# Two-layer trunk with a hierarchical mixture of experts: three quads' outputs exchanged by DRAM rows, and the routing instructions beside it

## The chip, the cores and the metric

The kernel runs on one core of one Trainium2 chip. The time is that of one execution in device microseconds; the time before is the median of three runs. The four engines that the text speaks of are TensorE (PE in the rows; PEld is its weight load), VectorE (DVE), ScalarE (ACT) and GpSimd (POOL); SyncE (SP) issues weight transfers.

## The reference, cut to what matters

Two trunk layers run one after the other. Layer 0 has 512 tokens (256 latent ones, 256 context ones) of width 1024; in layer 1 only the 256 latent tokens are left. Each layer ends in the mixture of experts that the change is about: every token picks one of four groups of experts and in it the best two of four experts.

```python
def hier_moe(h, w_grp, b_grp, w_rtr, b_rtr, w_gate, w_up, w_down):
    p_grp = jax.nn.softmax((h @ w_grp + b_grp).astype(jnp.float32), axis=-1)
    pg, g = lax.top_k(p_grp, 1)
    ...
    pe, ie = lax.top_k(jax.nn.softmax(logits_sel, axis=-1), TOP_K_IN_GROUP)
    wts = pg * pe / jnp.sum(pe, axis=-1, keepdims=True)
    eid = g * EXPERTS_PER_GROUP + ie
    gates = jnp.sum(jax.nn.one_hot(eid, N_EXPERTS, dtype=jnp.float32) * wts[..., None], axis=1).astype(h.dtype)
    y = jnp.zeros_like(h)
    for e in range(N_EXPERTS):
        a = jax.nn.silu(h @ w_gate[e]) * (h @ w_up[e])
        y = y + gates[:, e:e + 1] * (a @ w_down[e])
    return y
...
        out = hier_moe(jnp.concatenate([h2, h2c], axis=0), *moe_args)
        x = x + g2 * out[:B * N].reshape(B, N, D)
        xc = xc + cg2 * out[B * N:].reshape(B, L, D)
```

The residual streams are x (latent, `xl` in the kernel) and xc (context); g2 and cg2 are columns of `modT`.

## The kernel before, in words

The 16 experts are handled as four quads of four (one routing group each), in an order found at run time (`place`). A quad has slots instead of tokens: 64 for each expert make two slot tiles of 128, and a third tile takes what overflows, 32 more for each expert. The third tile is worked only if the quad has such tokens (`more[q] > 0`, the branch `beyond(q)`); with these inputs the second and the third quad have it.

The **routing gap** lies ahead of the experts. VectorE finds each token's two experts (`choose`), its rank among the tokens of that expert (`rk`) and from both the number of its slot (`Routing.slots`, L917), makes one-hot matrices `OH` of them (`one_hot`, L1060), and TensorE multiplies the normed tokens, split in a high and a low half (`h2h`, `h2l`), by OH to get the first quad's input `XT` (`gather`, L780). Most of these small VectorE instructions show line L89, that of a helper. The normed tokens are also written to DRAM, `h2d` (L778).

In `experts` (L1098) each quad runs through

- the gate and up phases: four weight chunks of 2 MB each (L1096 holds every expert matmul), in which the slots' columns are the stationary side and the weights are streamed; the results are in PSUM (`acc`, `aux`);
- `slots` and `fetch` (L1116, L1129): VectorE makes the slot table `SS` of a quad (for each slot the tokens that are in it, as 0 and 1) and from it the token number of each slot; POOL fetches those rows of h2d by indirect DMA (`xg`), and `turn` transposes them into the next quad's XT, PSUM being emptied half by VectorE, half by ScalarE (L1154);
- `gates` (L1169): each slot's factor;
- `down`: four weight chunks of 2 MB, in two halves of 512 columns; the outputs `da` stay in PSUM, slots by columns;
- `halves` and `combine` (L1293, L1312), the **exchange**: `da` is split into `oh` (ScalarE, L1299) and `ol` (VectorE, L1300), and TensorE multiplies both by the slot table SS (L1317), which turns slots into token columns and sums a token's two experts of the quad; `add` (L1328) adds the result into X with the modulation's factor. In quads 0 to 2 the first half's exchange stands between the second half's weight chunks, the second half's in the next quad's gate phase (`pending`).

The last quad of layer 0 does its down phase in three parts: columns 0 to 512 with two chunks, and 512 to 768 and 768 to 1024 with a column piece each (`columns`, L1106: two DMAs of 1 MB). In this text the four weight buffers of that phase are its first to fourth down piece.

All weights of a layer come on SP's queue into a ring of five buffers, with `slot0` as a sixth, each of 2 MB; a transfer is issued when the buffer that it overwrites has been read. The order on each engine is made by a scheduler, except for what `keep_in_program_order` pins (and what goes through `pinned(V)`).

Of the kernel before, what the change touches and what calls it, by code (L numbers as in the profile page):

```python
# [14 lines left out]
I32 = mybir.dt.int32  # L15
# [22 lines left out]
CAP = {0: 96, 1: 64}  # L38

# [4 lines left out]
CO_ID, CO_ONE, CO_TOK, CO_SLOT, CO_BEFORE, CO_BASE, CO_QUAD, CO_FIRST = 0, 128, 256, 768, 788, 804, 836, 840  # L44
CO_W = 844
# [11 lines left out]
def build(tc, ctx, a, cap=CAP):  # L57
# [9 lines left out]
    gd = dram.tile([T, 4], F32, name="gd")  # L67

# [101 lines left out]
    def transpose(out, in_):  # L170
        PE.transpose(out, in_, ident)  # L171
# [630 lines left out]
    class Route:  # L802


        def __init__(self, l, nt, small, rt):
            self.l, self.nt, self.rt = l, nt, rt
            self.small, self.used = small.tile([P, 130 * nt], F32, name="small"), 0
            self.vec = small.tile([P, 4, nt], F32, name="vec")
            self.gov = small.tile([P, nt, 16], F32, name="gov")
            self.flag = small.tile([P, 1], I32, name="flag")  # L810
            self.plan = small.tile([P, 8], I32, name="plan")
# [105 lines left out]
        def slots(self, rk):  # L917
# [14 lines left out]
                             m.rearrange("p (m c) -> p m c", c=16), axis=AX.X, op=ALU.add)  # L932

# [164 lines left out]
    def experts(l, nt, h2, vec, gov, fv, place, more, XT, xpool, pool, where, last, begun):  # L1098
# [45 lines left out]
        def turn(xg, XT):  # L1144

            for i in range(2):
                for st in range(nst):
                    tp = tmp()
                    for c in range(4):
                        transpose(tp[:, c * P:(c + 1) * P], xg[st][0][:, (i * 4 + c) * P:(i * 4 + c + 1) * P])  # L1150
                    d, s_ = XT[:, i * 4:i * 4 + 4, st * P:(st + 1) * P], tp.rearrange("p (c t) -> p c t", c=4)
                    if st % 2:
                        for c in range(4):
                            S.activation(d[:, c, :], s_[:, c, :], AF.Identity, bias=modT[0][:, 24 + i * 4 + c, 0:1])  # L1154
                    else:
                        V.tensor_tensor(d, s_, modT[0][:, 24 + i * 4:28 + i * 4, 0:1].to_broadcast([P, 4, P]), op=ALU.add)
                    yield
# [50 lines left out]
        if l == 0:  # L1208
            x8 = slot0[0].tile([P, 2048], F32, tag="x", name="x8")
            yg = itertools.cycle([x8[:, 1536:1792], x8[:, 1792:2048]])  # L1210
        pending = []
        sq = []
        quad = [0]
        for q in range(4):
# [4 lines left out]
            for ch in range(4):  # L1219
# [30 lines left out]
            elif q == 0:  # L1250
                gts = gates(0), gates(1)
                gt = gts[0]
# [40 lines left out]
            def halves(da, c0=0, c1=512, parts=None):  # L1293
# [13 lines left out]
                return parts  # L1307

# [38 lines left out]
            if q < 3:  # L1347
# [8 lines left out]
            else:  # L1356
# [4 lines left out]
                for c0, c1 in itertools.pairwise(cuts):  # L1361
# [6 lines left out]
                    else:  # L1368
# [6 lines left out]
                        down(da[hf], 0, w[:, :, :, c0 % 256:c0 % 256 + m], *cols)  # L1375
                    if ready:
# [17 lines left out]
    for l in range(L):  # L1394
# [79 lines left out]
        if l == 0:  # L1474
# [10 lines left out]
            rt.rows(rs)  # L1485
            place, more = ro.order()
# [29 lines left out]
        with phase(f"ex{l}") as pool:  # L1516
            where = itertools.cycle([ring] * 5 + ([spare] * EXTRA + early if l else slot0))
            nxt = experts(l, nt, None if l == 0 else h2, vec, gov, fv, place, more, XT, hp, pool, where, l == L - 1, begun)
# [6 lines left out]
def constants():  # L1525
# [14 lines left out]
    co[:, CO_FIRST:CO_FIRST + 4] = [-100, 1, 2, 3]  # L1540

# [103 lines left out]
```

## Time and profile before

| | |
|---|---|
| median of three runs | 918.75 us (917.89 to 919.88) |
| the profiled execution, whole | 920.78 us |
| its span in the trace | 919.0 us, mean granted clock 0.988 |
| layer 0's experts on TensorE | 248 to 541 us |
| bytes moved by DMA | 287.22 MB |

The rows further down come from the profiled execution, in microseconds from its span's start. In a row of the timeline the start and the duration come first, then the engine, the line, the operation, what it writes from what, how many like it follow at once, and in brackets the idle time before it and what ended it. In rows of waits the waiting engine and line stand left of the arrow, what it waited for right of it. PEq and SPq are the engines' sequencers.

### The profile page before, as it was taken

The page shows a single profiled execution, that of the slowest core. Times are in us where ns is not written, and L with a number is a line of the kernel's source. Part 1 is how long each engine was busy: PE and PEld are TensorE (multiplying, and loading weights), DVE is VectorE, ACT ScalarE, POOL GpSimd, SP SyncE. Part 2 cuts the span into 40 slices and gives each one's busy share as a digit, 9 for nine tenths or more (in the row PEclk, how much of TensorE's full clock was granted, in tenths as well). Part 3 has the DMA queues.
Part 4 walks back from the last instruction along what each step waited for, and adds up shares of the span by engine and source line. Part 5 has one row for each costly group of instructions (what it writes and reads, how often), then busy time and mean ns, then how long its engine had stood idle before and what let it go on. Part 6 is the DMA issues. An engine that isn't in the chain of part 4 may idle for free. (4 is left out here: it accounts for less than half of the span.)

```text
span 919.0 us, 13230 instructions
## 1 busy us (share of the span) xinstructions
PE 862.8 (94%) x5082; PEld 477.6 (52%) x5082; DVE 406.9 (44%) x1038; ACT 270.1 (29%) x598; POOL 59.5 (6%) x71
## 2 busy tenths in 40 slices
PE   3899999999998999999999989999999999979998
PEld 2588666676543323442343358666963444324435
DVE  1466677823875322240330159777553232212212
ACT  3344667514521100110120156567331111100101
POOL 1000000111010120011000020000000000000000
PEclk9999999999999999999999989999999999999999
DMA  9645663653989999679878945957969999999971
GB/s 358 283 179 208 257 267 115 251 227 112 385 342 430 424 422 428 257 270 409 333 284 345 326 161 224 425 245 280 361 276 358 417 431 426 428 406 431 424 247 47
DMA packets 33618, 287.22 MB, mean 313 GB/s; under 512 B 3580, under 2 KB 13564, under 8 KB 17024
## 3 DMA queue, kind: packets, MB, share of 16 engines
q1 hardware_dynamic: 29168, 276.94, 74.9%
q0 software_dynamic: 2400, 7.89, 2.2%
q10 hardware_dynamic: 1968, 1.32, 0.5%
q8 instruction: 49, 0.80, 0.3%
q14 instruction: 33, 0.27, 0.1%
HBM read 282.97 MB, written 3.16 MB: 311 GB/s over the span
## 5 line engine op out<-in xcount | busy, mean ns | idle before, releaser
L1096 PE MATMUL acc<-w,XT 128*64 128x512 f32 (+1 forms) x768 | 168.3, 600 | 7.4 <-PEq L998 5.8
L1096 PE MATMUL aux<-w,XT 128*64 128x512 f32 (+1 forms) x512 | 106.7, 593 | 0.6 <-PEq L1190 0.6
L1096 PEld LDWEIGHTS acc<-w,XT 128*64 128x64 f32 (+1 forms) x768 | 50.7, 133 | 106.2 <-issue 103.9
L1096 PEld LDWEIGHTS aux<-w,XT 128*64 128x64 f32 (+1 forms) x512 | 33.0, 130 | 66.0 <-issue 65.2
L1096 PE MATMUL acc<-w,x 128*64 128x512 f32 (+2 forms) x272 | 53.8, 574 | 2.6 <-PEq L1190 2.3
L192 PE MATMUL aux<-w,c 128*32 128x512 f32 x368 | 46.8, 625 | 0.0
L115 DVE TENSOR_TENSOR wl<-w,wh 128x768 fp32r<-128x768 f32 (+2 forms) x48 | 44.9, 977 | 2.0 <-PE aux L192 1.0
L1274 DVE SCALAR_TENSOR_TENSOR sg<-aux,gt,sg 128x512 f32<-128x512 f32 x12 | 9.0, 750 | 80.1 <-PE aux L1096 79.4
L1300 DVE TENSOR_TENSOR ol<-acc,oh 128x512 fp32r<-128x512 f32 (+1 forms) x25 | 15.7, 627 | 59.8 <-ACT oh L1299 59.7
L137 PE MATMUL acc<-wh,hh 128*128 128x512 f32 x96 | 38.8, 404 | 2.3 <-ACT hh L300 2.2
L1299 ACT CAST oh<-acc 128x512 fp32r<-128x512 f32 (+1 forms) x25 | 13.4, 535 | 93.5 <-PE acc L1096 93.4
L115 ACT CAST wh<-w 128x768 fp32r<-128x768 f32 (+2 forms) x48 | 37.5, 831 | 7.0 <-DMA w<-w_pf 3.9
L139 PE MATMUL acc<-wh,hl 128*128 128x512 f32 x96 | 38.8, 404 | 0.0
L138 PE MATMUL acc<-wl,hh 128*128 128x512 f32 x96 | 38.3, 399 | 0.0
L1239 ACT ACTIVATE sg<-acc 128x512 f32<-128x512 f32 x16 | 9.4, 597 | 87.0 <-PE acc L1096 86.7
L525 ACT ACTIVATE pr<-acc,soft 128x512 f32<-128x512 f32 (+1 forms) x48 | 29.5, 620 | 11.9 <-DVE soft L522 11.9
L1096 PEld LDWEIGHTS acc<-w,x 128*64 128x64 f32 (+1 forms) x272 | 15.5, 130 | 32.4 <-issue 31.6
L1154 ACT ACTIVATE XT<-tmp,modT 128x128 f32<-128x128 f32 x24 | 7.0, 368 | 78.3 <-PE tmp L171 78.2
L1096 PE MATMUL aux<-w,aT 128*64 128x512 f32 (+2 forms) x192 | 29.1, 453 | 0.0
L1096 PE MATMUL acc<-w,aT 128*64 128x512 f32 (+1 forms) x160 | 28.8, 511 | 0.2 <-DVE aT L1271 0.2
L574 PE MATMUL aux<-pT,vt 128*64 128x128 f32 x320 | 27.5, 282 | 0.1
L1082 PE MATMUL tmp<-OH,h 128*128 128x256 f32 x104 | 23.8, 383 | 2.5 <-DVE OH L1065 2.0
(322 smaller groups left out, 1555.6 us busy)
## 6 DMA issues: line engine op xcount, KB each, us to landing
w<-wg SPq DMA_DIRECT2D x32, 2048.0 KB, 12.8
w<-wu SPq DMA_DIRECT2D x32, 2048.0 KB, 11.6
w<-wd SPq DMA_DIRECT2D x29, 2048.0 KB, 12.9
w<-w_mod SPq DMA_DIRECT2D x23, 2048.0 KB, 10.1
w<-w_out SPq DMA_DIRECT2D x4, 2048.0 KB, 7.8
w<-wd SPq DMA_DIRECT2D x6, 1024.0 KB, 12.8
w<-w_qkv SPq DMA_DIRECT2D x3, 1536.0 KB, 9.3
w<-w_pf SPq DMA_DIRECT2D x2, 2048.0 KB, 8.4
```

Of the source, the lines that this page charges most:

```text
L115: return S.copy(hi, x), eng.tensor_tensor(lo, x, hi.bitcast(F32), op=ALU.subtract)
L137: PE.matmul(out, lhs[0], rhs[0], start=start, stop=False, skip_group_check=True)
L138: PE.matmul(out, lhs[0], rhs[1], start=False, stop=False, skip_group_check=True)
L139: PE.matmul(out, lhs[1], rhs[0], start=False, stop=stop, skip_group_check=True)
L192: mm = PE.matmul(m[32 * j:32 * j + 32, :], sc2[:, k, :], w[:, kk, j * 512:(j + 1) * 512], start=(ch == chs[0] and kk == 0), stop=(ch == ch ...
L525: S.activation(pr[e], sp[e], AF.Exp, bias=nm[:, e:e + 1], scale=SCALE, accum_out=sums[:, e:e + 1])
L574: PE.matmul(o[e * 64:(e + 1) * 64, c * P:(c + 1) * P], vt[:, k0 + m, e * 64:(e + 1) * 64], pTs[e * nk + m], start=(m == 0), stop=(m == nk ...
L1082: PE.matmul(y[:, :W], x[:, tt, k * P:(k + 1) * P], OH[tt][:, c0:c1], start=(i == 0 and tt == 0), stop=(x is h2[-1] and tt == nt - 1))
L1096: PE.matmul(o, lhs[:, c0:c0 + m], w[:, j, :], start=(k == 0), stop=(k == last_k), skip_group_check=True)
L1239: S.activation(t, ga[st], AF.Silu)
L1299: S.copy(oh, da[st][:, c0:c1])
L1300: V.tensor_tensor(ol, da[st][:, c0:c1], oh.bitcast(F32), op=ALU.subtract)
```

## The change

In layer 0, quads 0 to 2 lose `halves` and `combine`. In their place `store` copies each of the three slot tiles' outputs from PSUM (ScalarE, for the second tile VectorE) and POOL's queue writes 256 KB for each and each half to rows of a DRAM tensor `yd`, six for a quad; a quad without third tile writes its first tile there instead. Row q x 384 + slot holds a slot's output, row 1152 zeros. In the routing gap `places` works out, for each token and each of its two experts, the number of that row; an expert of the last quad, or none, gives the row of zeros.

In the last quad's down phase `collect` fetches the two rows of each token, 128 tokens at a time, with two indirect DMAs of 512 KB, adds them on VectorE, transposes the sum in eight pieces on TensorE and adds them into X: the first two tiles of tokens around columns 0 to 512, the other two around columns 512 to 768. The last quad's own outputs go through `halves` and `combine` as before.

Also: quad 0 gets no slot table; the tables of the quads behind the second are pinned; the second quad's gates are written later; `turn` empties PSUM by VectorE alone.

```diff
 def slots(self, rk):
...
+            if l == 0:
+                self.ranks = self.rt.work[:, 560:560 + nt * 16]
+                S.copy(self.ranks, rk[:, 0:nt * 16])
+
+        def places(self):
...
+            V.tensor_tensor(b, self.base, c16[1], op=ALU.add)
+            V.tensor_scalar(t, r, 64.0, None, op0=ALU.is_ge)
+            V.tensor_tensor(t, t, c16[0][:, None, :].to_broadcast([P, nt, 16]), op=ALU.mult)
+            V.tensor_tensor(t, t, r, op=ALU.add)
+            V.scalar_tensor_tensor(t, self.ov, 1e6, t, op0=ALU.mult, op1=ALU.add)
+            V.tensor_tensor(t, t, b[:, None, :].to_broadcast([P, nt, 16]), op=ALU.add)
+            V.tensor_tensor(m.rearrange("p (i t) c -> p i (t c)", i=2), self.M.rearrange("p (i t) c -> p i (t c)", i=2),
+                            t.rearrange("p t c -> p (t c)")[:, None, :].to_broadcast([P, 2, nt * 16]), op=ALU.mult)
+            V.tensor_reduce(f, m, axis=AX.X, op=ALU.add)
+            V.tensor_scalar(self.rows, f, float(YD), None, op0=ALU.min)
...
-                V.tensor_scalar(t, bc[0], s_, None, op0=ALU.is_equal)
+                i = V.tensor_scalar(t, bc[0], s_, None, op0=ALU.is_equal)
+                if l == 0 and q > 1:
+                    tc.keep_in_program_order(i)
...
-                    if st % 2:
-                        for c in range(4):
-                            S.activation(d[:, c, :], s_[:, c, :], AF.Identity, bias=modT[0][:, 24 + i * 4 + c, 0:1])
-                    else:
-                        V.tensor_tensor(d, s_, modT[0][:, 24 + i * 4:28 + i * 4, 0:1].to_broadcast([P, 4, P]), op=ALU.add)
+                    V.tensor_tensor(d, s_, modT[0][:, 24 + i * 4:28 + i * 4, 0:1].to_broadcast([P, 4, P]), op=ALU.add)
...
+            z = pool.tile([P, D], F32, tag="xg", name="z", bufs=3)
+            G.memset(z[0:1, :], 0.0)
+            G.dma_start(yd[YD:YD + 1, :], z[0:1, :])
+        def collect(tts):
+
+            for tt in tts:
+                g = [pool.tile([P, D if tag == "xg" else nst * 512], F32, tag=tag, name="yr", bufs=3 if tag == "xg" else 2)[:, 0:D]
+                     for tag in (("xg", "xg"), ("oh", "ol"), ("xg", "SS"), ("xg", "xg"))[tt]]
+                for i in range(2):
+                    G.indirect_dma_start(out=g[i], out_offset=None, in_=yd[:, :],
+                                         in_offset=bass.IndirectOffsetOnAxis(ap=places[:, i * nt + tt:i * nt + tt + 1], axis=0))
+                tc.keep_in_program_order(V.tensor_tensor(g[0], g[0], g[1], op=ALU.add))
+                for i in range(2):
+                    t = tmp()
+                    for c in range(4):
+                        tc.keep_in_program_order(
+                            transpose(t[:, c * P:(c + 1) * P], g[0][:, (i * 4 + c) * P:(i * 4 + c + 1) * P]))
+                    for c in range(4):
+                        k = i * 4 + c
+                        x = X[tt // 2][:, k, tt % 2 * P:tt % 2 * P + P]
+                        V.scalar_tensor_tensor(x, t[:, c * P:(c + 1) * P], modT[l][:, 40 + k, tt // 2:tt // 2 + 1], x,
+                                               op0=ALU.mult, op1=ALU.add)
...
-                    SS, _ = slots(0, False)
+                    SS = None if l == 0 else slots(0, False)[0]
...
-                gts = gates(0), gates(1)
-                gt = gts[0]
+                gt = gates(0)
...
+            if l == 0 and q == 0:
+                gts = gt, gates(1)
...
+            def store(da, hf):
+
+                ys = pool.tile([P, nst, 512], F32, tag=("oh", "ol")[hf], name="ys", bufs=2)
+
+                def put(st, y):
+                    r0 = q * 384 + st * P
+                    G.dma_start(yd[r0:r0 + P, hf * 512:(hf + 1) * 512], y)
+
+                for st in range(2):
+                    (V.tensor_copy if st else S.copy)(ys[:, st, :], da[st])
+                    put(st, ys[:, st, :])
+                with beyond(q) as there:
+                    S.copy(ys[:, 2, :], da[2])
+                    put(2, ys[:, 2, :])
+                with there.Else():
+                    put(2, ys[:, 0, :])
...
-            if q < 3:
+            if l == 0 and q < 3:
+                for hf in range(2):
+                    for c in range(2):
+                        down(da[hf], 2 * c, weights(wd(l, place[q], 2 * hf + c)))
+                    store(da[hf], hf)
+            elif q < 3:
...
+                    if l == 0 and c0 < 768:
+                        collect(range(c0 // 256, c0 // 256 + 2))
...
             rt.rows(rs)
+            ro.places()
             place, more = ro.order()
```

**TensorE, first quad's down phase.** Before, ahead of and inside the second half's weights (x is the activations' transpose; xg the fetched rows; a branch row is that of the third tile):

```order
L1096 MATMUL acc<-w,x_2503 64x512 x8
L171 MATMUL tmp<-co,xg 128x128 x3
L1317 MATMUL tmp<-SS,oh 128x512
L1317 MATMUL tmp<-SS,ol 128x512
L1317 MATMUL tmp<-SS,oh 128x512
L1317 MATMUL tmp<-SS,ol 128x512
L1322 COMPARE_AND_BRANCH
```

And with the change, the same place:

```order
L1124 MATMUL acc<-w,x_2515 64x512 x7
L1370 COMPARE_AND_BRANCH
L1370 UNCONDITIONAL_BRANCH x2
L1124 MATMUL acc<-w,x_2515 64x512
L173 MATMUL tmp<-co,xg 128x128
L1124 MATMUL acc<-w,x_2515 64x512 x2
L1124 MATMUL aux<-w,x_2515 64x512 x2
```

The exchange's matmuls are gone from between the weight matmuls, and nothing takes their place there.

**TensorE, last quad's down phase with the change**, from the second down piece to the first exchange (yr is the sum of two fetched rows):

```order
L1124 MATMUL acc<-w,x_2515 64x512 x8
L173 MATMUL tmp<-co,yr 128x128 x8
L1124 MATMUL acc<-w,x_2515 64x256 x2
L1124 MATMUL aux<-w,x_2515 64x256 x2
...
L1124 MATMUL aux<-w,x_2515 64x256
L173 MATMUL tmp<-co,yr 128x128 x8
L1124 MATMUL aux<-w,x_2515 64x256
L1384 MATMUL acc<-SS,oh 128x512
```

The first token tile's eight transposes stand ahead of the third down piece, the second's inside it; the third's and the fourth's follow among the exchange's matmuls, ahead of the fourth piece.

**POOL, from the third quad's last stores on, with the change** (ys is the stored copy):

```order
L1365 DMA yd<-ys 128x512 x2
L1246 DMA yr<-yd,rows 128x1024 x4
L917 TENSOR_LOAD plan
L1216 COMPARE_AND_BRANCH
L1216 UNCONDITIONAL_BRANCH x2
L1246 DMA yr<-yd,rows 128x1024 x2
...
L1246 DMA yr<-yd,rows 128x1024
...
L1246 DMA yr<-yd,rows 128x1024
```

Six of the eight fetches follow the stores at once; the last token tile's two come one by one, the second of them after the first tile's transposes have freed the buffer that it is written to.

**VectorE, routing gap, with the change** (L951 to L957 are of `places`; small and rw are its work space):

```order
L91 TENSOR_SCALAR small<-acc 128x64
L951 TENSOR_TENSOR rw<-rw,co 128x16
L91 SCALAR_TENSOR_TENSOR rw<-small,rw 128x64
...
L952 TENSOR_SCALAR rw<-rw 128x64
L91 TENSOR_REDUCE vec<-rw 128x8
L953 TENSOR_TENSOR rw<-rw,co 128x64
L91 TENSOR_SCALAR sj<-names,vec 128x256
L954 TENSOR_TENSOR rw<-rw 128x64
L91 SCALAR_TENSOR_TENSOR OH<-names,vec,sj 128x256
...
L955 SCALAR_TENSOR_TENSOR rw<-small,rw 128x64
```

Four of the nine instructions stand ahead of the first one-hot matrix, the others between the later ones; seven are ahead of the last piece of h2l.

## Rows read from the trace of the kernel before

**Rows 1.** The page, part 1: busy time and share of the span.

```profile
PE 862.8 (94%) x5082; PEld 477.6 (52%) x5082; DVE 406.9 (44%) x1038; ACT 270.1 (29%) x598; POOL 59.5 (6%) x71
```

**Rows 2.** Table by stretch: us, TensorE busy (instructions), granted clock, DMA share, GB/s.

```profile
276.00:523.00 247.00, 236.40 (x1268) 1.00 0.90 361
288.00:317.00 29.00, 25.56 (x112) 1.00 1.01 428
448.00:484.00 36.00, 35.65 (x195) 1.00 0.72 277
```

**Rows 3.** Waits, TensorE, 276 to 523 us: total, times, longest us.

```profile
PE acc L1096 <- PEq L1190: 1.8, 4, 0.5
```

**Rows 4.** Waits, SP's DMA queue, 240 to 545 us.

```profile
SPq L108 <- PE acc L1096: 88.5, 15, 11.6
SPq L108 <- PE aux L1096: 85.5, 17, 11.0
```

**Rows 5.** Table by stretch, of L1317, the exchange matmuls, alone (PE, then weight loads).

```profile
299.70:321.40 21.70, 9.77 (x32) 5.39 (x32) 1.00 1.01 426
377.70:404.40 26.70, 12.38 (x48) 8.62 (x48) 1.00 0.68 261
461.40:488.10 26.70, 12.39 (x48) 8.61 (x48) 1.00 0.68 260
```

**Rows 6.** Groups by form, 276 to 545 us: busy us, mean ns of one.

```profile
L1156 DVE TENSOR_TENSOR XT<-tmp,modT 128x512 f32<-128x512 f32 x12 | 8.0, 689 | 17.2 <-PE tmp L171 17.2
...
L1299 ACT CAST oh<-acc 128x512 fp32r<-128x512 f32 x13 | 7.6, 586 | 44.1 <-PE acc L1096 44.1
L1174 DVE SCALAR_TENSOR_TENSOR sk<-bc,co,bg 128x1024 f32<-128x1024 f32 x6 | 7.4, 1279 | 0.2 <-DVEq L1278 0.2
...
L1154 ACT ACTIVATE XT<-tmp,modT 128x128 f32<-128x128 f32 x24 | 7.0, 368 | 78.3 <-PE tmp L171 78.2
...
L1337 DVE SCALAR_TENSOR_TENSOR xl<-tmp,modT,xl 128x256 f32<-128x256 f32 x12 | 5.8, 481 | 9.0 <-PE tmp L1317 9.0
```

**Rows 7.** Timeline, TensorE: start, us, instruction.

```profile
363.42 1.06 PE L171 MATMUL tmp<-co,xg 128*128 128x128 f32 x8 [0.83 <-PE tmp L171]
```

**Rows 8.** Timeline, TensorE in the routing gap.

```profile
239.07 2.14 PE L791 MATMUL acc<-OH,h2h 128*128 128x256 f32 x16 [1.83 <-DVE OH L89]
...
248.19 2.37 PE L1096 MATMUL acc<-w,XT 128*64 128x512 f32 x10
```

**Rows 9.** Timeline, VectorE in the routing gap.

```profile
235.32 0.17 DVE L89 TENSOR_SCALAR rw<-tmp 128x16 f32<-128x16 f32 x1 [0.42 <-PE tmp L858]
...
237.73 0.29 DVE L89 TENSOR_REDUCE vec<-rw 128x8 f32<-128x128 f32 x1
```

**Rows 10.** Timeline, POOL.

```profile
253.59 0.76 POOL L778 DMA_DIRECT2D h2d<-xt  x1 [0.51 <-DVE small L89]
267.59 1.43 POOL L1140 DMA_INDIRECT xg<-h2d,ii  x1 [13.24 <-PEq L1190]
```

**Rows 11.** Line L778, the write of h2d: its landing.

```profile
DMA to landing us min/median/max: 7.4/8.6/9.7
```

**Rows 12.** Timeline, TensorE, end of the last quad.

```profile
523.63 0.60 PE L1096 MATMUL aux<-w,x 128*64 128x256 f32 x4
...
532.30 0.65 PE L1096 MATMUL acc<-w,x 128*64 128x256 f32 x4
...
543.89 1.16 PE L270 MATMUL acc<-co,part 128*128 128x1 f32 x8 [2.55 <-POOL part L261]
```

**Rows 13.** Timeline, SP, the last quad's column pieces.

```profile
502.51 12.29 SPq L1110 DMA_DIRECT2D w<-wd  x4
```

**Rows 14.** Line L1140, the indirect fetches: landing.

```profile
DMA to landing us min/median/max: 9.8/16.0/22.3
```

**Rows 15.** Table by stretch: all engines, granted clock behind the last quad.

```profile
545.00:551.50 6.50, 5.38 (x25) 3.64 (x24) 3.80 (x9) 1.42 (x3) 0.00 (x0) 0.50 0.00 0
```

**Rows 16.** Timeline, TensorE, transposes of the first fetched tiles.

```profile
293.07 1.06 PE L171 MATMUL tmp<-co,xg 128*128 128x128 f32 x8 [1.37 <-DMA xg<-h2d,ii]
```

More of the change, by code (lines that the diff above doesn't have):

```diff
@@ L38 @@
 CAP = {0: 96, 1: 64}
+YD = 3 * 384
 PAR_BMOD, PAR_NG, PAR_WR, PAR_BR, PAR_PSC = 0, 96, 128, 448, 488
 PAR_W = 492
-CO_ID, CO_ONE, CO_TOK, CO_SLOT, CO_BEFORE, CO_BASE, CO_QUAD, CO_FIRST = 0, 128, 256, 768, 788, 804, 836, 840
-CO_W = 844
+CO_ID, CO_ONE, CO_TOK, CO_SLOT, CO_BEFORE, CO_BASE, CO_QUAD, CO_FIRST, CO_ROW = 0, 128, 256, 768, 788, 804, 836, 840, 844
+CO_W = 876
 MC_ROT, MC_MASK = 0, 512
@@ L67, in build @@
     gd = dram.tile([T, 4], F32, name="gd")
+    yd = dram.tile([YD + 1, D], F32, name="yd")
     def phase(name, side="left"):
@@ L170, in transpose @@
     def transpose(out, in_):
-        PE.transpose(out, in_, ident)
+        return PE.transpose(out, in_, ident)
     def keep_warm(n, bank=tmp):
@@ L810, in __init__ @@
             self.flag = small.tile([P, 1], I32, name="flag")
+            self.rows = small.tile([P, 2 * nt], I32, name="rows") if l == 0 else None
             self.plan = small.tile([P, 8], I32, name="plan")
@@ L932, in slots @@
                              m.rearrange("p (m c) -> p m c", c=16), axis=AX.X, op=ALU.add)
+            if l == 0:
+                self.ranks = self.rt.work[:, 560:560 + nt * 16]
+                S.copy(self.ranks, rk[:, 0:nt * 16])
+        def places(self):
+            nt = self.nt
+            c16 = [co[:, CO_ROW + i * 16:CO_ROW + (i + 1) * 16] for i in range(2)]
+            r = self.ranks.rearrange("p (t c) -> p t c", t=nt)
+            w = self.rt.work[:, 324:]
+            b = w[:, 0:16]
+            t = w[:, 16:80].rearrange("p (t c) -> p t c", t=nt)
+            m = w[:, 80:208].rearrange("p (m c) -> p m c", c=16)
+            f = w[:, 208:208 + 2 * nt]
+            V.tensor_tensor(b, self.base, c16[1], op=ALU.add)
[8 more added lines that the diff above has]
+            V.tensor_scalar(self.rows, f, float(YD), None, op0=ALU.min)
         def gates(self):
@@ L1096, in step, with experts @@
             PE.matmul(o, lhs[:, c0:c0 + m], w[:, j, :], start=(k == 0), stop=(k == last_k), skip_group_check=True)
-    def experts(l, nt, h2, vec, gov, fv, place, more, XT, xpool, pool, where, last, begun):
+    def experts(l, nt, h2, vec, gov, fv, place, more, places, XT, xpool, pool, where, last, begun):
         n = nt * P
@@ L1517, in build @@
             where = itertools.cycle([ring] * 5 + ([spare] * EXTRA + early if l else slot0))
-            nxt = experts(l, nt, None if l == 0 else h2, vec, gov, fv, place, more, XT, hp, pool, where, l == L - 1, begun)
+            nxt = experts(l, nt, None if l == 0 else h2, vec, gov, fv, place, more, ro.rows, XT, hp, pool, where, l == L - 1, begun)
         hp_stack.close()
@@ L1540, in constants @@
     co[:, CO_FIRST:CO_FIRST + 4] = [-100, 1, 2, 3]
+    j = np.arange(16) % 4
+    co[:, CO_ROW:CO_ROW + 16] = 192 - 32 * j
+    co[:, CO_ROW + 16:CO_ROW + 32] = -32 * j - 1
     mc = np.zeros((P, MC_W), f)
```

## The prediction

> **What bounds the kernel now.** Read the busy times first: TensorE works 862.8 of 919.0 us [rows 1]. That average hides which stretch matters, so the next view is the table by stretch. Layer 0's experts (276 to 523 us, from the first quads up to the last quad's column pieces) keep TensorE busy 236.40 of 247 us while the DMA engines are 0.90 busy and move 361 GB/s [rows 2]. So there are two near limits: TensorE on top, the DMA engines close below. They saturate only early: 428 GB/s at a share of 1.01 between 288 and 317 us, but 277 GB/s (0.72) between 448 and 484 [rows 2]. Which of the two holds? TensorE's largest group of waits in that stretch is 1.8 us in total, at branches, not for a weight [rows 3], while SP, which issues the weights, spends 88.5 and 85.5 us waiting until TensorE has read out a buffer of the ring [rows 4]. Hence TensorE sets the pace here, and a microsecond of matmuls taken away is a microsecond gained until the DMA engines are full.
>
> **What goes.** Quads 0 to 2 lose their exchange matmuls. Three windows hold their blocks, and in them the exchange line alone is busy 9.77, 12.38 and 12.39 us (32, 48 and 48 matmuls; the middle quads have a third slot tile) [rows 5]: **-34.5 us** on TensorE. Nothing hides it, since these matmuls stand between the weight matmuls in TensorE's own queue. What hung on them (the splitting, the additions into X) ran on other engines; the copies that replace the split cost one ScalarE copy of 0.59 us instead of a copy and a subtraction [rows 6], so a PSUM bank comes free no later. Gone as well is quad 0's slot table, three pairs of instructions on VectorE, for which nobody waits there: nothing. The transposes' evacuation moves from ScalarE (four of 0.37 us per bank) to VectorE (one of 0.69 us) [rows 6]: shorter per bank, hidden, nothing. Deferring the second quad's gate factors and pinning the later tables leave TensorE's queue alone: nothing.
>
> **What comes on TensorE.** 32 transposes of 128x128. Eight took 1.06 us [rows 7], so 4 x 1.06 = **+4.3 us**. All stand in the last quad's down phase.
>
> **What comes in the routing gap.** Nine small VectorE instructions and a ScalarE copy. VectorE is the engine that TensorE waits for there (1.83 us for the one-hot matrix OH [rows 8]), and its chain is dense: its row at 235.32 us has only 0.42 us idle ahead of it [rows 9]. The order shows seven of the nine ahead of the last piece of h2l. Neighbours take 0.17 us (128x16) to 0.29 us (128x128) [rows 9]; with the step from one to the next 7 x 0.26 gives **+1.8 us**. Bounds: 0, if all fall into the gaps that h2l's matmuls leave, and 9 x 0.33 = 3.0. I take 1.8, as nothing in the order leaves that chain. h2d's second write, which now stands behind the plan's load on POOL, is read by the first fetch 14 us after it was issued (253.59 against 267.59) [rows 10] and lands in 7.4 to 9.7 us [rows 11]: hidden, unless it is over 4 us later.
>
> **What comes on the DMA engines.** 18 stores of 256 KB (4.72 MB) and eight fetches of 512 KB (4.19 MB), 8.9 MB in all, on POOL's queue beside the weights. The stretch moved 361 GB/s x 247 us = 89.2 MB [rows 2], which is 208 us at 428. The 8.9 MB add 20.9 us: 229 us of work in 247. So the last weights can come at best 247 - 229 = 18 us earlier, at 506 instead of 523.6, or at 503.5 if the last tile's fetches (1.05 MB, 2.5 us) go behind them. The third down piece is 2.1 MB ahead of the fourth; at some 330 GB/s, what fetches in between leave to the weights, that is 6.4 us: 497.1. TensorE would ask for it at 523.63 [rows 12] - 34.5 + 1.06 = 490.2. That leaves a wait of **+6.9 us**. Bounds: 0 (the engines had slack before the stretch too, and the fetches need not come in front), and 13 us if the last pieces come apart by the 12.29 us that SP took to issue the four of them [rows 13] instead of 6.4.
>
> **The collecting chain.** The last tile's second fetch can only be issued behind the first tile's transposes, as the POOL order shows: between 489 us, where TensorE first comes to them, and 497; I take 493. Issuing takes 1.43 us [rows 10]; landing takes 9.8 to 22.3, median 16.0 us [rows 14]; adding the two fetched halves is a 128x1024 VectorE instruction, whose nearest row is 1.28 us [rows 6]. That gives 505.5 at the minimum, 511.7 at the median. TensorE wants these transposes at 497.1 + (532.30 - 523.63) [rows 12] = 505.8. So the wait is 0 to 5.9 us; with 32 small updates of X (each below the 0.48 us of a 128x256 one [rows 6]), of which the second tile's eight stand behind the third tile's addition on VectorE, I take **+4 us**. Range 0 to 12 (22.3 instead of 16.0).
>
> [...]
>
> **The sum.** -34.5 + 4.3 + 1.8 + 6.9 + 4 + 1 = -16.5 us. The profiled execution took 920.78 us, 2.0 above the median of the runs, 918.75; so 904.3 for such a run, 902.2 for the median: **902 us**. Layer 1 and all ahead of 230 us keep their times.
>
> [...]
>
> **Rivals.**
> 1. *All transfers hide.* TensorE stays the only bound: -34.5 + 4.3 + 1.8 = -28.4, **890 us**. For it: the share of 0.72 at 448 to 484 us [rows 2], SP's long waits [rows 4]. Against it: 8.9 MB need 20.9 us more while the stretch shrinks by 30. It needs both waits to vanish. Chance 0.13.
> 2. *The fetches land fast, the weights stay the limit.* The collecting term is 0: -20.5, **898 us**. For it: the minimum of 9.8 us [rows 14] would be in time; the fetch comes when few weights are left. Chance 0.14.
> 3. *The transfers eat most of the gain.* Weights 13 and collecting 5 us, routing 3, clock 3: -34.5 + 4.3 + 24 = -6.2, or -12 where the first is 7 as taken above: **907 to 913 us**. For it: a fetch's median landing of 16.0 us under load [rows 14] and the dense queue at 1.01 early on [rows 2]. Against it: the share of 0.72 later. Chance 0.18.
> 4. *Slower: the fetches starve behind the weights.* The first three fetches, 1.57 MB, were issued from 267.59 us [rows 10], and TensorE waited for them until 293.07 [rows 16]: 62 KB/us, while all queues together moved 428 [rows 2]. If the third quad's last stores and all eight fetches (5.0 MB) went at that rate from 448 us (its exchange began at 461.4 [rows 5], less the 22 us taken out ahead, and some 9 us of weights follow), they would end at 529, and with a landing of some 10 us at 539, against 505.8 where the last tile is wanted: a wait of 33 in place of 4, so -34.5 + 4.3 + 1.8 + 6.9 + 33 + 1 = +12.5, **931 us**. It decides from a wait of 20.5 us, a rate of some 73 KB/us. Against it: the weights are nearly all in by 506, after which nothing stands in the way. Chance 0.07.
> 5. *No change that can be measured*, by smaller misfortunes of 3 and 4 together: **918 us**. Chance 0.03.
>
> [...]
>
> **How the numbers follow.** The forecast has 0.45, the rivals 0.13, 0.14, 0.18, 0.07 and 0.03. A measurement can tell 0.2% (1.8 us) from no change. Faster by more: 0.45 + 0.13 + 0.14 + 0.18 = 0.90; slower by more: 0.07; within it 0.03. The forecast's own range, with the two waits between their ends, is 896 to 908. Taking in rivals 1 to 3 gives 889 to 913, which leaves out rivals 4 and 5 and thin edges of the rest, between 1 and 2 in 10.
>
> **What would show it.** No exchange blocks between 299 and 488 us, and a down phase of each early quad shorter by 10 to 12 us. The DMA share near 1.0 from some 281 to 505 us. A wait of about 7 us of TensorE on a weight transfer ahead of the last quad's third down piece, and one of about 4 on yr (its addition or its fetch) in the last two tiles. The first weight matmuls at about 250 instead of 248.2 us. From the last exchange on, the same stages as before, shifted. Wrong would be: TensorE waits on yr of 15 us and more (rival 4), no wait at all in the last quad (rival 1), waits on weights spread over quads 1 and 2 rather than in the last, which says that the stores displace the weights when they are issued, or a routing gap that shrinks.

## The result and the profile after

The changed kernel takes 909.85 us (median of four runs, 908.33 to 911.67) against 919.32 us for the kernel before beside it (four runs): ratio 0.9900, 95% interval 0.9883 to 0.9916. That is 9.5 us faster, where 17 us were forecast: outside the forecast's own range (896 to 908 us), inside the 889 to 913 us that take in three of its rivals, and where rival 3 stands (907 to 913). The profiled executions' spans are 919.0 and 909.8 us; the account below goes by these 9.2 us.

The page's busy times, after:

```profile
PE 843.1 (93%) x4986; PEld 463.1 (51%) x4986; DVE 399.6 (44%) x1040; ACT 252.8 (28%) x554; POOL 69.0 (8%) x84
```

Beside [rows 1], TensorE is busy 19.7 us less, and the span is shorter by less than half of that: time left as work and came back as waiting and as slower work. The table by stretch shows where the DMA engines now stand (columns as in [rows 2]):

```profile
281.00:431.00 150.00, 140.95 (x801) 0.99 1.01 427
431.00:456.00 25.00, 23.82 (x152) 1.00 0.97 382
456.00:500.00 44.00, 39.43 (x184) 1.00 1.02 422
502.20:508.60 6.40, 5.08 (x23) 0.50 1.09 397
516.90:522.70 5.80, 5.80 (x21) 0.51 0.72 308
```

The DMA engines are full from 281 to 520 us (shares of 0.97 to 1.09), but for a stretch at 382 GB/s; before, 277 GB/s was all that 448 to 484 us needed [rows 2]. In the last two rows, both in the last quad, TensorE's granted clock is 0.50 and 0.51, in the rows above 0.99 and 1.00. TensorE's waits, 240 to 560 us (total, times, longest):

```profile
PE acc L1124 <- DMA w<-wd: 5.3, 3, 3.6
PE acc L272 <- POOL part L263: 4.2, 1, 4.2
PE tmp L173 <- DVE yr L1248: 3.2, 1, 3.2
PE acc L1124 <- PEq L1026: 2.7, 1, 2.7
...
PE acc L290 <- DVE ii L1165: 1.5, 1, 1.5
```

The first and the third (the weights, and the last tile's sum) are the waits that the prediction had. The fourth, at the branch around the overflow work, and the last, for VectorE's row numbers in the first quad, it had not. The second stands behind the last exchange, for `part`, the sums of squares for the next norm; before, it was 2.55 us [rows 12]. The last quad on TensorE's timeline:

```profile
492.77 3.65 PE L1124 MATMUL acc<-w,x 128*64 128x512 f32 x16 [0.46 <-DMA w<-wd]
496.35 1.09 PE L173 MATMUL tmp<-co,yr 128*128 128x128 f32 x8
501.00 0.65 PE L1124 MATMUL acc<-w,x 128*64 128x256 f32 x4 [3.56 <-DMA w<-wd]
...
502.52 1.07 PE L1124 MATMUL aux<-w,x 128*64 128x256 f32 x4
504.90 1.12 PE L1124 MATMUL acc<-w,x 128*64 128x256 f32 x4 [1.31 <-DMA w<-wd]
...
516.89 1.97 PE L173 MATMUL tmp<-co,yr 128*128 128x128 f32 x8 [3.19 <-DVE yr L1248]
...
532.25 0.73 PE L1384 MATMUL acc<-SS,ol 128*128 128x512 f32 x2 [0.40 <-DVE ol L1350]
537.22 1.87 PE L272 MATMUL acc<-co,part 128*128 128x1 f32 x8 [4.24 <-POOL part L263]
```

The third down piece starts at 501.00 us. Before, it started at 523.20: the row at 523.63 in [rows 12] is its second four matmuls, and its first four are the last of the twenty in the first row below, a step of 0.43 us earlier. Four of its matmuls take 0.65 us before the clock falls (501.00) and 1.07 behind it (502.52). The exchange ends at 532.98 (532.25 + 0.73). Before, it ended at 541.35, by the row of its last matmul:

```profile
519.72 4.09 PE L1096 MATMUL acc<-w,x 128*64 128x512 f32 x20 [0.46 <-PEq L1190]
...
540.95 0.40 PE L1317 MATMUL acc<-SS,ol 128*128 128x512 f32 x1
```

So 22.2 us are gained at the third piece, and 13.8 of them are lost behind it. TensorE's busy time in that stretch, before and after:

```profile
523.20:541.35 18.15, 16.63 (x98) 1.00 0.62 252
```

```profile
501.00:532.98 31.98, 26.48 (x120) 0.79 0.66 262
```

That loss is what the experiments had to explain. Behind it, 1.9 us more are lost between the last exchange and layer 1's first matmuls (13.5 us instead of 11.6). Layer 1 from there on is 2.7 us shorter than in the profile before (363.3 instead of 366.1 us); the kernel before without the overflow branch of layer 0 (below) has 363.1 too, so these 2.7 us are not the change's.

### The profile page after: what moved, and what is told of

It reads as the page before. It is cut to its first block, busy times and chain, and to the rows that moved or that the text cites. A ratio compares the mean times of both kernels' runs of the same rounds, so it can differ in the third digit from the quotient of the medians.

```text
span 909.8 us, 12910 instructions
## 1 busy us (share of the span) xinstructions
PE 843.1 (93%) x4986; PEld 463.1 (51%) x4986; DVE 399.6 (44%) x1040; ACT 252.8 (28%) x554; POOL 69.0 (8%) x84
## 5 line engine op out<-in xcount | busy, mean ns | idle before, releaser
L1124 PE MATMUL acc<-w,XT 128*64 128x512 f32 (+1 forms) x768 | 171.9, 609 | 11.0 <-PEq L1026 7.4
L1124 PE MATMUL acc<-w,x 128*64 128x512 f32 (+2 forms) x272 | 56.2, 592 | 5.9 <-DMA w<-wd 5.3
L1368 ACT COPY ys<-acc 128x512 f32<-128x512 f32 x6 | 3.5, 585 | 126.2 <-PE acc L1124 126.2
L1349 ACT CAST oh<-acc 128x512 fp32r<-128x512 f32 (+1 forms) x14 | 6.9, 494 | 86.6 <-PE acc L1124 52.1
L1124 PE MATMUL aux<-w,x 128*32 128x512 f32 (+2 forms) x144 | 25.9, 565 | 0.0
## 6 DMA issues: line engine op xcount, KB each, us to landing
w<-wd SPq DMA_DIRECT2D x29, 2048.0 KB, 16.5
yd<-ys POOLq DMA_DIRECT2D x18, 256.0 KB, 11.6
```

The lines of the kernel that those rows point to most:

```text
L1124: PE.matmul(o, lhs[:, c0:c0 + m], w[:, j, :], start=(k == 0), stop=(k == last_k), skip_group_check=True)
```

## The experiments

Each ratio is to the kernel before on the same chip, with its 95% interval; a gain over the changed kernel is the difference to 0.9900.

**The overflow branch.** Ahead of the third quad's gate phase all engines pass a branch around the work for tokens that fit no slot. TensorE's wait there is 2.66 us, before it was 0.73. No token of these inputs needs that work. The branch left out of layer 0, the same edit to both kernels:

```diff
-                if ch == 1 and q == 2:
+                if l and ch == 1 and q == 2:
                     overflow(l, nt, h2, gov, fv, pool)
```

Expected of the changed kernel without it:

> The changed kernel without the overflow branch of layer 0 (with these inputs no token needs it, so no arithmetic is left out for them; for other inputs tokens beyond the slots would be). In the changed kernel TensorE waits 2.66 us at that branch and then works at a granted clock of 0.75 for 6.8 us. Theory C (what TensorE loses in waits and at the lower clock comes out at the end): the wait and the clock give back 2.7 to 4.4 us, some 905.5 to 907 us. Theory D (the DMA engines, full from 281 to 520 us, bring the last weights and rows when they do): the time saved at 385 us is lost again ahead of the last quad's third down piece, whose start stays at about 501 us; 909 to 910 us.

Expected of the kernel before without it:

> The kernel before without the overflow branch of layer 0 (none of these tokens needs it). Control for the same edit in the changed kernel, which gave 5.5 us. Cover theory (the exchange matmuls queued ahead of the branch hid the load of its flag; TensorE waited only 0.73 us and its clock stayed at 1.00): 0 to 1 us, 917.5 to 918.5 us. Rival (the branch costs every engine the same in both kernels): 4 us or more, under 914.5 us.

Measured: 0.9847 (0.9818 to 0.9876), 904.3 us, a gain of 4.9 us; and 0.9982 (0.9969 to 0.9995), 917.3 us, a gain of 1.7. By the medians the branch costs the changed kernel some 3 us more than the kernel before; the intervals together are as wide as that. Theory D fell here: the third piece came 3.4 us sooner too (497.58 us), and the DMA engines carried 429 GB/s about where they had carried 382:

```profile
427.00:452.00 25.00, 24.65 (x152) 1.00 1.01 429
```

Then the branch kept, but with work of TensorE's put ahead of it:

```diff
-                if ch == 1 and q == 2:
+                if l == 0 and ch == 0 and q == 2:
+                    for _ in range(2):
+                        keep_warm(1)
+                if ch == int(l > 0) and q == 2:
                     overflow(l, nt, h2, gov, fv, pool)
```

> The changed kernel with the overflow branch kept but moved behind the third quad's first eight gate matmuls (two small matmuls on constants, one to each transpose bank, hold it there), so that TensorE has 3.6 us of work queued while the branch's flag is loaded. Cover theory: the wait of 2.66 us and the fall of the clock at 385 us vanish as in the run without the branch, 904 to 906 us. Rival (what the run without the branch gained came from the other engines' branches): 908 us or more.

Measured: 0.9874 (0.9855 to 0.9893), 907.2 us, between the two expectations, and the interval overlaps the changed kernel's. The wait did not go: it is 2.45 us. The clock stayed at 1.00 (380 to 395 us), but that is not shown to be the edit's. It stayed there in the runs with the last tile's own buffer and with the nine instructions late, which have the branch in its old place and waits of 2.4 and 2.6 us at it:

```profile
380.00:395.00 15.00, 12.59 (x72) 1.00 1.01 423
```

```profile
380.00:395.00 15.00, 12.40 (x72) 1.00 1.02 424
```

In the changed kernel and in six other runs with the branch it is 0.89 in that stretch, so after waits of this size both were seen.

What lasts is not the flag's load but the branch itself. The line of the branch, engine TensorE's sequencer (times min/median/max in ns, first and last start), before, after, and with the branch moved:

```profile
L998 PEldq COMPARE_BRANCH  x2: 3561/5016/6471, 400.2 to 801.4; - x2
```

```profile
L1026 PEldq COMPARE_BRANCH  x2: 6171/6306/6441, 378.5 to 794.2; - x2
```

```profile
L1026 PEldq COMPARE_BRANCH  x2: 5836/6080/6324, 381.6 to 789.1; - x2
```

Of each two, one is layer 0's (the first start) and one layer 1's. In the kernel before, layer 0's takes 3.56 us (400.2 to 403.7), where the DMA engines move 183 GB/s; after, 6.44 (378.5 to 384.9), at 430; moved, 5.84 (381.6 to 387.4). Layer 1's, at 419 GB/s before, took 6.47. In these rows the busy times of TensorE's weight load, VectorE, ScalarE and GpSimd stand behind TensorE's:

```profile
399.00:405.00 6.00, 5.27 (x24) 1.88 (x22) 1.18 (x4) 0.00 (x0) 1.01 (x2) 1.00 0.44 183
800.00:808.00 8.00, 3.01 (x21) 1.97 (x17) 1.75 (x4) 0.47 (x1) 0.73 (x1) 0.97 1.00 419
```

After (TensorE alone):

```profile
378.00:385.00 7.00, 4.45 (x21) 1.00 1.02 430
385.20:392.00 6.80, 6.80 (x30) 0.75 1.01 421
```

The flag's load beside it takes 0.31 us in all. What TensorE still had queued when its sequencer came to the branch, before, after and moved:

```profile
403.87 0.40 PE L1317 MATMUL aux<-SS,ol 128*128 128x512 f32 x1
```

```profile
381.43 1.02 PE L1124 MATMUL acc<-w,XT 128*64 128x512 f32 x2
```

```profile
385.55 0.39 PE L179 MATMUL tmp<-count 128*128 128x256 bf16 x2
388.39 8.08 PE L1124 MATMUL acc<-w,XT 128*32 128x512 f32 x52 [2.45 <-DVE sj L1151]
```

That work ends at 404.27, 382.45 and 385.94 us, so each time it covers some 4 us from the branch's start (4.1, 4.0 and 4.3). The exchange's going did not take that cover away, and matmuls put ahead of the branch did not lengthen it, as the sequencer came to the branch 3.1 us later. It is the branch that became longer, and then some 4 us cover the shorter one and not the longer. (With the branch moved it ends at 387.4, 1.5 us into the wait; the profile puts the rest to a VectorE instruction.) The stores and fetches are not needed for it: the branch takes 6.42 us in the kernel before without exchange, which has neither, and 6.26 in the changed kernel without fetches (both below). The DMA engines move 417 GB/s in the first (376 to 384 us) and 422 in the second (380 to 395).

What the branch does in this time no run shows. The rows show 3.56 us beside 183 GB/s and 5.84 to 6.47 beside 416 to 430; with the branch moved, 416 in 382 to 389 us. Behind the longer wait the clock of the changed kernel's profile stands at 0.75 for 6.8 us of matmuls: 1.7 us lost, an estimate (a quarter of the 6.8).

**The last quad's clock.** The same kernel with work in TensorE's two longest waits:

```diff
+    def warm_into(bank, n):
+        for _ in range(n):
+            tc.keep_in_program_order(PE.matmul(bank, count[:, 0:P], count, start=True, stop=True, skip_group_check=True))
...
+                if tt in (0, 2):
+                    warm_into(bank[:, tt * 128:tt * 128 + 256], 16 if tt else 20)
```

> The changed kernel with 20 small matmuls on constants behind the first fetched tile's transposes and 16 behind the third's, where TensorE waits 3.6 and 3.2 us: they keep it at work there and write to a bank that is overwritten. Theory C: the granted clock stays at 1.00 from 500 to 533 us instead of 0.58 to 0.90, and the time falls by 4 to 5 us, to some 905. Theory D: the last tile's second fetch lands at 515 us whatever TensorE does, so only what stands behind it runs faster: 1 to 3 us, 907 to 909 us.

Measured: 0.9821 (0.9800 to 0.9842), 902.8 us, a gain of 7.3 us by adding work. In the last quad its clock stays at 1.00 until 524 us, where the changed kernel's fell twice (the rows from 502.20 and 516.90 above):

```profile
500.50:524.00 23.50, 21.19 (x130) 1.00 0.89 354
...
529.51 1.87 PE L276 MATMUL acc<-co,part 128*128 128x1 f32 x8 [2.26 <-POOL part L267]
```

The third piece started 0.5 us sooner (500.48 us), so nearly the whole gain lies behind it: theory C, and more than it asked. But it is not all the clock's. From the third piece to the last exchange the run takes 26.8 us instead of 32.0. The matmuls on constants behind the third piece take 1.7 us of that, its waits 2.1 instead of 4.9, and the other work some 4 us less. The waits fell in part because the order changed too: the last tile's transposes stand behind five of the exchange's matmuls now. Another 2.0 us came behind the last exchange, where the wait for `part` is 2.26 us instead of 4.24. No run tells these shares apart.

**The transfers.** The fetches left out, and then the stores as well:

```diff
-                    G.indirect_dma_start(out=g[i], out_offset=None, in_=yd[:, :],
-                                         in_offset=bass.IndirectOffsetOnAxis(ap=places[:, i * nt + tt:i * nt + tt + 1], axis=0))
+                    G.memset(g[i], 0.0)
...
-                    G.dma_start(yd[r0:r0 + P, hf * 512:(hf + 1) * 512], y)
+                    if hf < 0:
+                        G.dma_start(yd[r0:r0 + P, hf * 512:(hf + 1) * 512], y)
```

> The changed kernel with the eight fetches of stored rows replaced by writing zeros on POOL: the first three quads' outputs never reach X, the additions and transposes stay. 4.19 MB, 9.8 us of full DMA engines, go away, and with them the wait for the last tile. Theory D: no wait of TensorE on weights or rows in the last quad, no fall of the clock there: 3.6 + 1.3 + 3.2 us of waits and some 4 us of clock, 896 to 899 us. Theory C alone would keep the waits on weights (5 us): 903 us or more.

> The changed kernel without the stores of the first three quads' outputs and without the fetches (zeros instead): the copies, additions and transposes stay, 8.9 MB of transfers go. Without the fetches alone it took 902.9 us. If the stores hold back the weights of the second and third quad (TensorE waited 1.3 us for weights in the second): 900 to 901.5 us. If they were hidden: 902.5 to 903.5 us. What is then left over the run of the kernel before without exchange (889.4 us) is work in the last quad and the routing gap, some 11 us: transposes 4.3, VectorE's order 3.2, routing 1.4, clock.

Measured: 0.9829 (0.9798 to 0.9860), 902.9 us, and 0.9768 (0.9729 to 0.9806), 899.9 us (four runs, 895.2 to 903.7). The wait on weights is gone in both, as theory D has it (the third piece at 497.13 and 496.39 us, without a wait), but the first gain is 6.5 us and not 11 to 14. The stores' part, 3 us by the medians, is not told from none, as the intervals overlap; what is left over the run without exchange below (889.4 us) is 10.6 us, the 11 expected. What stayed is seen in the first of them:

```profile
509.26 1.97 PE L173 MATMUL tmp<-co,yr 128*128 128x128 f32 x8 [3.19 <-DVE yr L1247]
```

```profile
505.67 0.61 DVE L1256 SCALAR_TENSOR_TENSOR xc<-tmp,modT,xc 128x128 f32<-128x128 f32 x2 [1.54 <-PE tmp L173]
506.44 1.64 DVE L1256 SCALAR_TENSOR_TENSOR xc<-tmp,modT,xc 128x128 f32<-128x128 f32 x6 [0.15 <-DVEq L1354]
508.00 1.21 DVE L1247 TENSOR_TENSOR yr<-yr 128x1024 f32<-128x1024 f32 x1
```

TensorE waits the same 3.19 us for the last tile although nothing is fetched: VectorE does the third tile's eight updates of X (0.61 + 1.64 us) and only then the last tile's addition. In the changed kernel, too, the addition stands right behind these updates (515.62 us), and the last fetch, issued at 497.7 us, had landed 6.5 us later, at 504.2. The wait was never the fetch's, and the 515 us that an expectation above gives for its landing is wrong.

**The last tile.** Its own buffer, and then also the additions first:

```diff
-                     for tag in (("xg", "xg"), ("oh", "ol"), ("xg", "SS"), ("xg", "xg"))[tt]]
+                     for tag in (("xg", "xg"), ("oh", "ol"), ("xg", "SS"), ())[tt]]
+                if tt == 3:
+                    t = xpool.tile([P, KD, W], F32, tag="XT", name="yr", bufs=1).rearrange("p k t -> p (k t)")
+                    g = [t[:, 0:D], t[:, D:2 * D]]
```

> The changed kernel with the last token tile's two fetches written to the buffer of XT, which is free when the last up phase ends (487 us), so that their issue no longer waits for the first tile's transposes (492.8 and 497.7 us). Chain theory: the fetches land some 8 us earlier, the wait of 3.2 us ahead of the last tile's transposes goes, and with it part of the lower clock: 3 to 5 us, 905 to 907 us. Theory D: the 1.05 MB only come in front of the last weights instead of behind them; the third down piece starts 2.5 us later, and the sum changes by under 2 us: 908 to 911 us.

Measured: 0.9897 (0.9877 to 0.9916), 909.4 us: nothing. The last fetches were issued at 485.8 and 487.1 us instead of 492.8 and 497.7; the wait of 3.19 us stayed, and the wait ahead of the third piece grew from 3.56 to 5.31 us:

```profile
501.51 1.12 PE L1124 MATMUL acc<-w,x 128*64 128x256 f32 x4 [5.31 <-DMA w<-wd]
...
516.18 1.09 PE L173 MATMUL tmp<-co,yr 128*128 128x128 f32 x8 [3.19 <-DVE yr L1251]
```

Theory D names what happens, but not its size: with the fetches brought forward the third piece starts 0.5 us later (501.51 instead of 501.00), not 2.5. The rest of the longer wait is that TensorE came to it 1.2 us sooner, with its clock at 1.00 behind the branch in this execution. With the order of VectorE changed as well:

```diff
+            got = []
             for tt in tts:
...
                 tc.keep_in_program_order(V.tensor_tensor(g[0], g[0], g[1], op=ALU.add))
+                got.append((tt, g))
+            for tt, g in got:
                 for i in range(2):
```

> The changed kernel with XT's buffer for the last tile's fetches, and with both tiles' additions written ahead of both tiles' transposes and updates of X. The wait of 3.19 us ahead of the last tile's transposes was the same in the run without any fetch, so VectorE's order (the third tile's eight updates ahead of the last tile's addition) should be its cause. VectorE theory: that wait falls to 1.5 us or less (the transposes then still need two banks free), and with the clock kept up 2 to 4 us go, 905.5 to 907.5 us. Landing theory: the wait stays near 3 us, and 909 to 910 us.

Measured: 0.9852 (0.9824 to 0.9880), 906.0 us, a gain of 4.4 us, where the buffer alone had given 0.3 (the two intervals just overlap). In place of 3.19 us TensorE waits 1.03 and twice 0.38, for transpose banks, and behind the last exchange 2.39 us for `part` instead of 4.24:

```profile
513.39 0.66 PE L173 MATMUL tmp<-co,yr 128*128 128x128 f32 x4 [1.03 <-DVE xc L1263]
514.43 0.66 PE L173 MATMUL tmp<-co,yr 128*128 128x128 f32 x4 [0.38 <-DVE xc L1263]
...
533.11 1.87 PE L272 MATMUL acc<-co,part 128*128 128x1 f32 x8 [2.39 <-POOL part L263]
```

**The routing gap.** The nine instructions moved behind the chain, each pinned to its place there:

```diff
             rt.rows(rs)
-            ro.places()
...
             ro.gates()
+            ro.places()
```

> The changed kernel with the nine instructions that find the rows' numbers pinned behind the routing chain, after the gate factors, so that they no longer stand ahead of the one-hot matrices. Routing theory: the first weight matmuls start 1.4 us sooner against the instructions ahead of them, 908 to 909 us. Rival (the 1.4 us are waited for again at the last quad's third down piece, which the transfers bring): the start moves and the time doesn't, 909.5 to 910.5 us.

Measured: 0.9860 (0.9836 to 0.9883), 907.0 us, against 0.9900 (0.9883 to 0.9916): the intervals touch, so that it is faster by the nine instructions' time is not shown. Their price on VectorE is in the traces. From the reciprocal that starts the chain to the first one-hot matrix it takes 7.25 us with the nine in between and 7.16 with them late; to the last group of h2l 12.74 and 12.57. After, and with the nine late:

```profile
230.53 0.18 DVE L280 RECIPROCAL rs<-rs 128x4 f32<-128x4 f32 x1 [1.44 <-ACT rs L279]
...
236.02 0.17 DVE L951 TENSOR_TENSOR rw<-rw,co 128x16 f32<-128x16 f32 x1
236.14 0.23 DVE L91 SCALAR_TENSOR_TENSOR rw<-small,rw 128x64 f32<-128x64 f32 x1
...
237.78 0.48 DVE L91 SCALAR_TENSOR_TENSOR OH<-names,vec,sj 128x256 fp32r<-128x256 f32 x1
...
243.27 2.74 DVE L769 SCALAR_TENSOR_TENSOR h2l<-xt,rs,h2h 128x512 fp32r<-128x512 f32 x4
```

```profile
230.40 0.18 DVE L280 RECIPROCAL rs<-rs 128x4 f32<-128x4 f32 x1 [1.44 <-ACT rs L279]
...
237.56 0.48 DVE L91 SCALAR_TENSOR_TENSOR OH<-names,vec,sj 128x256 fp32r<-128x256 f32 x1
...
242.97 2.73 DVE L769 SCALAR_TENSOR_TENSOR h2l<-xt,rs,h2h 128x512 fp32r<-128x512 f32 x4
```

So the nine cost 0.1 to 0.2 us there. The kernel before without branch or without exchange, which has none of them, takes 7.16 us to the first one-hot matrix too; the kernel before takes 7.43. More goes with TensorE's clock from 238 to 242 us: 1.00 before and with the nine late, 0.67 after. The first sixteen matmuls on OH take 2.14, 2.14 and 3.01 us in these three, the next four 1.02, 1.02 and 1.79. But the clock is 0.68 and 0.64 in the kernel before without branch and without exchange, so the nine are not needed for the lower clock, and no run shows what brings it.

**The removal by itself.** The kernel before, the exchange of three quads left out and nothing added:

```diff
-            if q < 3:
+            if l == 0 and q < 3:
+                for hf in range(2):
+                    for c in range(2):
+                        down(da[hf], 2 * c, weights(wd(l, place[q], 2 * hf + c)))
+                    halves(da[hf])
+            elif q < 3:
```

> The kernel before with the exchange of quads 0 to 2 left out and nothing in its place: their outputs are split but never reach X. It prices the removal by itself, without stores, fetches, transposes or the instructions in the routing gap. If the 35 us of exchange were all on TensorE's path and nothing took their place: 883.5 us. With the wait at the overflow branch uncovered and the clock that falls behind it (4.4 us): some 888 us. If the weights alone now held TensorE up (89.2 MB at 428 GB/s are 208 us, against 247 - 35 = 212): 890 us or more, with waits on weights in the trace.

Measured: 0.9680 (0.9661 to 0.9698), 889.4 us, 29.9 us gained of 34.5. From the first weight matmul to the third down piece TensorE is busy 33.4 us less, before and in this run:

```profile
248.19:523.20 275.01, 263.39 (x1396) 1.00 0.89 357
```

```profile
248.61:493.46 244.85, 229.99 (x1268) 1.00 0.98 397
```

TensorE waited 3.5 us at the same branch (6.4 us long there too, at 417 GB/s) and 2.2 for gate weights. The clock stayed at 1.00 in 380 to 395 us.

**Edits together.** Branch moved, own buffer, additions first, nine instructions late; then also the matmuls on constants (20 and 8):

> Four edits to the changed kernel together: the branch behind eight gate matmuls, XT's buffer for the last tile, additions ahead of transposes, rows' numbers behind the routing chain. If their gains (2.7, 3.8 and 0 to 1.4 us) add up: 902 to 903.5 us. If the weights' arrival takes the first and the last back: 904.5 to 906 us.

> The same four edits and the small matmuls on constants in the two waits of the last quad (20 and 8). The run with the matmuls alone gained 7.0 us. If that gain is the clock's and adds to the others: 895 to 898 us. If the edits have taken the same waits already: 900 to 903 us.

Measured: 0.9852 (0.9824 to 0.9881), 907.1 us, and 0.9818 (0.9790 to 0.9845), 903.6 us. The gains don't add. In these two the third piece starts at 501.85 and 502.34 us, later than in the changed kernel, behind waits of 4.84 and 1.91 us for the weights: their arrival takes the early gains back, and what is left lies behind it. Of the versions that do the whole work, the changed kernel with only the matmuls on constants is as fast as any, 902.8 us.

## Why the prediction was right, and where its sum was off

The direction held, and so did the main claim: exchange matmuls stood on TensorE's path. The size did not: the sum said -16.5 us, -9.5 were measured, nearly 2 us beyond the forecast's own range. The terms, forecast and measured in the profiled execution (us):

| term | forecast | measured |
|---|---|---|
| exchange matmuls | -34.5 | -33.4 when removed alone; 29.9 net there, by the medians |
| transposes at full clock | +4.3 | 4 x 1.06 = +4.2 |
| routing gap | +1.8 | +0.1 to 0.2 by the nine; the first weight matmul 0.9 later (249.12 us), beside the clock of 0.67 |
| weights, last quad | +6.9 (0 to 13) | 3.56 + 1.31 = +4.9 |
| collecting | +4 (0 to 12) | 3.19 + 0.40 = +3.6, by another cause |
| clock | +1 | 1.7 at the branch, an estimate; 6.7 in the last quad |
| branch | none | 2.66 - 0.73 = +1.9 |
| other waits in quads 0 and 1 | none | 1.46 + 0.73 + 1.25 = +3.4 |

The last quad's clock is TensorE's busy time there, 26.48 us, less the 16.63 before and three tiles' transposes of 1.06. The two stretches at 0.50 and 0.51 make up some 5.4 of the 6.7, an estimate: half of their busy 5.08 and 5.80 us. With 0.9 for the routing gap the sum of the right column is -6.1; it misses 1.15 us that the first fetch gained (it was waited for 1.37 us before [rows 16], 0.22 after) and two waits of 0.46 and 0.47 at branches behind the third piece, which are gone: some -8.2, where the last exchange ended 8.4 us sooner. Behind it 1.9 us were lost, where the prediction had the same stages as before, and 2.7 came in layer 1 that are not the change's: 9.2 us in all.

- **The step that failed is the clock's**, +1 us in the sum. No run shows that term; the runs showed 1.7 us at the branch, an estimate, and 6.7 in the last quad. There the clock fell twice, for some 6 us each: to 0.50 at 502.2 to 508.6 us, behind the wait of 3.56, and to 0.51 at 516.9 to 522.7, behind that of 3.19. Both fell mostly on work (TensorE busy 5.08 of 6.40 us and 5.80 of 5.80). Without the fetches the first wait is gone and with it the first fall (1.00 from 495 to 505 us); the second stays: 0.77 from 505 to 520 us, the transposes behind the wait in 1.97 us, the eight ahead of it in 1.03. With matmuls on constants in both waits neither came (1.00 from 500.5 to 524 us), and the kernel was 7.3 us faster, some 4 of them in the work of this stretch.
- **The branch** was the step missing. It had as much cover as before, some 4 us of queued matmuls, but lasted 6.44 us instead of 3.56; the early quads without exchange have the DMA engines at 430 GB/s there instead of 183.
- **The routing gap**: here a chain without idle time was not a chain without room. Most of its instructions use the result of the one before; after, those at 234.77, 234.98 and 235.18 us start 0.21 and 0.20 us apart, though each takes 0.16 or 0.17. The nine, whose results none of them uses, went in between: 0.12 us from the start of one of the nine to the chain's next (236.02 and 236.14). In all they cost 0.1 to 0.2 us.
- **Collecting** had the right size by luck: of the two halves of that step the landing played no part, the order on VectorE, named in half a sentence, was all of it.
- **Weights** came near the forecast, 4.9 us for 6.9, but both ends of that wait were off: TensorE was there at 497.4 us instead of 490.2, the third piece at 501.0 instead of 497.1. The 490.2 also rests on 523.63 as the piece's start before, which was 523.20.
- Rival 4 (fetches that starve): a fetch landed in 6.5 to 18.3 us, median 16.6, about as before [rows 14], and no wait of TensorE's was theirs. Rival 1 fell by the waits of 4.9 us. Rivals 2 and 3 each had a part: landing didn't matter, and 907 to 913 is where it came out, yet by clock and branch more than by the weights.

## What to carry to other kernels

When matmuls were taken out of this busy stretch, the transfers beside it moved closer together, and a branch beside them took longer: the DMA engines went from 183 to 430 GB/s there, and the branch from 3.56 us to 6.44. A wait of TensorE's is to be priced together with the work behind it: here two waits, 6.8 us together, were followed by 6.7 us of slower work. Where a wait can't be removed, work that is thrown away may be worth its place: here 36 matmuls on constants came with a gain of 7.3 us. And before a late operand is blamed on its transfer, run the kernel without the transfer: here the wait was 3.19 us with the fetches and without.

## What was not expected of the hardware

The branch on TensorE's sequencer takes 3.56 us at 183 GB/s and 5.8 to 6.5 us in all other rows, at 416 to 430 GB/s where the rate was read; only one branch met little traffic, so the dependence rests on that one. After waits of 2.4 to 3.5 us at the branch the clock fell in some runs (0.89 in 380 to 395 us) and not in others (1.00), with the branch in its old place as well as moved; why stays open. So does why four edits together gain no more than the additions' order alone: the runs of one kernel spread over 1.7 to 8.5 us, and no run separates their parts.
